# ScalarE takes the decode's gate sums and maxima out of the shared PSUM bank, and VectorE reads the copies

## The chip, the cores and the metric

The kernel runs on one NeuronCore of a Trainium2 chip. Its engines are TensorE (PE in the profile, with its weight loads as PEld), VectorE (DVE), ScalarE (ACT), GpSimd (POOL), which here mostly issues gathers, and SyncE (SP), which issues DMAs. Each engine works through its own instructions in order and waits at semaphores for the others. The metric is the device time of one execution in microseconds (us), the median of several runs; lower is better.

## What is computed

One step of a one-layer decoder for two groups that share their weights: a prompt of 1024 rows and a sample of 8 rows, each of which has 64 pages of 128 cached keys and values behind it. The work that the change touches is the forgetting attention of the sample over its cache:

```
c = jnp.cumsum(lf_all, axis=1)          # running sums of the forget gates' logs
s = jnp.einsum('bqhd,bkhd->bhqk', q, k) * (ATT_HEAD_DIM ** -0.5)
s = s + (cq - ck)                       # gate sum of the query less that of the key
p = jax.nn.softmax(s, axis=-1)
out = jnp.einsum('bhqk,bkhd->bqhd', p, v)
```

Around it the reference computes, for both groups, the input projection with RMSNorm, the prompt's causal attention with the same gates, a chunked spatial gating, an output projection, cross-attention into 256 memory rows, a gated MLP with a causal convolution, and the final norm; caches and states are returned too. All of it is float32.

## The kernel before

The prompt is the main line: input projection (`p1`), attention of rows 0 to 511 and of rows 512 to 1023 (`attention(0)`, `attention(1)`), then for each half output projection, cross-attention and MLP (`mid`, `ffn`). Float32 products are made of three matmuls on split operands (L272 to L274): ScalarE rounds a weight tile into `wh` (L235) and VectorE computes the rest `wl` (L236).

The sample's work is mixed into that line as a background generator, at a pace set per stage (`PACE`). `decode()` goes through 8 batches of 16 steps: a step gathers a 1 MB tile of keys through POOL (L1420), VectorE multiplies and sums it (L1436/L1440, or L1427/L1428 while the prompt's attention runs) into the scores `s`; two steps behind, the batch before gets its values gathered (L1482) and multiplied on TensorE (L1488). Keys and values share four `kv` buffers. Once for each batch:

- step 13: `gates` sums the gates. TensorE multiplies the page totals `tot` by a triangle (L1410) into a tile of 128x8, and VectorE makes the decay `dec` of 128x512 from that tile and the scanned gates `A` (L1412).
- step 15: `soft_max` adds `dec` to `s` (L1452) and takes each row's maximum `pm` (L1454).
- step 0 of the next batch: `soft_all` transposes `pm` (L1460), takes the maximum over all (L1463, L1464) and writes it on a diagonal `dg` (L1466).
- step 1 of the next batch: `soft_exp` spreads the maxima over the partitions with a matmul by ones (L1473) into a tile of 128x8, VectorE subtracts that tile from `s` (L1475), ScalarE takes the exponential (L1476) and VectorE sums it (L1477).

PSUM's eight banks are given out so: four `ba` and two `bb` for the main line, one `dv` for the decode's value sums, and one `ms`. `ms` holds a single buffer. The decode's small products (L1410, L1460, L1473) go there, and so does every third tile of the prompt attention's transposes and value products (`B3`: L836, L852, L872), which ScalarE copies out (L843, L861). A new tile in `ms` waits until all readers of the last one are done.

The order of instructions on each engine is made when the program is built: a planner simulates the engines' time and takes what is ready by priority. `tc.high_priority()` puts a block ahead of others in that choice; `behind(ENG.PE)` puts the decode's matmuls behind TensorE's newest instruction. At run time the order is fixed.

Of the kernel before, what the change touches and what calls it, by code (L numbers as in the profile page):

```python
# [11 lines left out]
AF = mybir.ActivationFunctionType  # L12
ALU = mybir.AluOpType
# [5 lines left out]
P = 128  # L19
# [59 lines left out]
def build(nc, tc, ctx, a, phases=None):  # L79
# [27 lines left out]
    def nm(s):  # L107
        cnt[0] += 1
        return f"{s}_{cnt[0]}"
# [16 lines left out]
    def sm(shape, tag, bufs=2, dt=F32):  # L126
        return small.tile(shape, dt, tag=tag, bufs=bufs, name=nm(tag))
# [24 lines left out]
    def MS():  # L152
        return BB() if MB else psum.tile([P, 512], F32, tag="ms", bufs=1, name=nm("ms"))
# [1207 lines left out]
    def behind(e):  # L1361

        return tc.issue_after(last[e]) if e in last else nullcontext()


    def decode():
# [36 lines left out]
        def gates(b, A):  # L1403
            tot = sm([P, 8], "tot", 2)
            nc.vector.tensor_tensor(
                tot, A.rearrange("p (h k) -> p h k", k=64)[:, :, 63], lfz[:, b * 8 : b * 8 + 8], op=ALU.add
            )
            ps = MS()
            with behind(ENG.PE):
                mmul(ps[:, :8], suf, tot, start=True, stop=True)  # L1410
            dt_ = dec("dec").rearrange("p (k h) -> p k h", h=8)
            nc.vector.tensor_tensor(  # L1412
                dt_, ps[:, :8].unsqueeze(1).broadcast_to((P, 64, 8)), A.rearrange("p (h k) -> p k h", k=64), op=ALU.subtract
            )
            return dt_

# [52 lines left out]
        def soft_exp(b, st, dg):  # L1469
            s = st[1]  # L1470
            ps = MS()
            with behind(ENG.PE):
                mmul(ps[:, :8], ones, dg, start=True, stop=True)  # L1473
            with tc.high_priority():
                nc.vector.tensor_tensor(s, s, ps[:, :8].unsqueeze(1).broadcast_to((P, 64, 8)), op=ALU.subtract)  # L1475
                nc.scalar.activation(s, s, AF.Exp)  # L1476
                nc.vector.tensor_reduce(lps[:, b, :], s.rearrange("p k h -> p h k"), axis=AX.X, op=ALU.add)  # L1477

# [38 lines left out]
        st, A, dt_, pm, dg, dv, vm = ([None] * 8 for _ in range(7))  # L1517
        pend = []
        st[0] = prep(0)
        for g in range(8 * 16 + 16 + VLAG + 2):  # L1520
# [5 lines left out]
            if ch == 1 and 1 <= b < 9:  # L1526
                soft_exp(b - 1, st[b - 1], dg[b - 1])
            left = 1
            if b < 8:
                left = yield from kstep(b, ch, st[b])  # L1530
                if ch == 11:
                    A[b] = gates_scan(b)
                if ch == 13:
                    dt_[b] = gates(b, A[b])
                if ch == 14 and b < 7:
                    st[b + 1] = prep(b + 1)
                if ch == 15:
                    pm[b] = soft_max(b, st[b], dt_[b])
# [486 lines left out]
```

## Time and profile before

| | us |
|---|---|
| runs of the kernel before: 1794.02, 1795.83, 1805.24; median | 1795.83 |
| the profiled execution's own time | 1805.72 |
| its span, first to last instruction | 1803.8 |
| TensorE busy in it | 1743.2 |
| VectorE busy | 1399.9 |
| ScalarE busy | 733.9 |
| GpSimd busy | 504.2 |

The profiled execution's time is its span and 1.92 us around it, and it lies 9.89 us above the median, near the longest of the three runs. By time of the span, the prompt's input projection ends near 275 us, the two attentions run from about 275 to 495 us, the first half's output projection, cross-attention and MLP follow to about 1100 us, and the second half's to the end. The decode's last value product is near 1416 us; after it comes the sample's own projection, cross-attention and MLP.

An answer of the trace gives for an instruction or a group its start, its duration, its engine and line, what it writes and reads, and in brackets the idle time of the engine just before it with what ended that. "x2" at a row's end means two instructions of the kind. A group's row has its count, its busy time and the mean of one in ns, then the engine's idle time before them by what ended it.

### The profile page before, as it was taken

To read this page: it belongs to the slowest core of one execution; us is meant where nothing else is said; L and a number is where in the kernel's file an instruction comes from. 1 tells how busy PE (TensorE), PEld (TensorE's weight loads), DVE (VectorE), ACT (ScalarE), POOL (GpSimd) and SP (SyncE) were. 2 spreads that over 40 slices of the span, in tenths; PEclk is the share of its full clock that TensorE was granted. 3 is DMA by queue.
4 is the path that set the end of the run, shared out by engine and by line. 5 is a ranking of instruction groups with operands and counts; after the bars stand their busy time and mean duration, and the time that the engine had idled before them with its cause. 6 is when DMAs were issued, how large, how long until landed. Compare 5 with 4: busy or idle time off the path is not lost.

```text
span 1803.8 us, 25097 instructions
## 1 busy us (share of the span) xinstructions
PE 1743.2 (97%) x9637; PEld 1291.8 (72%) x9637; DVE 1399.9 (78%) x1733; ACT 733.9 (41%) x1374; POOL 504.2 (28%) x461
## 2 busy tenths in 40 slices
PE   8999999878999999999999999999999999999997
PEld 5887777656677767777777777766666778767875
DVE  4689658987789897999999999887885549855344
ACT  6332256465634634433333244235353323332332
POOL 1252333432233433233232232433432112102110
PEclk9999999998999999999999999999999999999999
DMA  7886888786597986788788788988888677568982
GB/s 293 301 297 224 303 317 330 259 272 198 193 406 277 353 337 249 269 301 338 293 297 313 295 310 308 374 295 325 312 312 323 238 290 254 186 261 298 358 311 82
DMA packets 157074, 521.06 MB, mean 289 GB/s; under 512 B 20874, under 2 KB 40842, under 8 KB 124186
## 3 DMA queue, kind: packets, MB, share of 16 engines
q0 software_dynamic: 57168, 341.14, 50.0%
q1 hardware_dynamic: 92874, 165.73, 26.3%
q10 hardware_dynamic: 6912, 12.59, 1.9%
q8 instruction: 76, 1.25, 0.3%
q14 instruction: 44, 0.36, 0.1%
HBM read 495.47 MB, written 23.93 MB: 288 GB/s over the span
## 4 chain that ended last, share of the span: by engine, by line
PE 41%; issue 12%; DMA 10%; DVE 7%; POOL 4%; ACT 1%; POOLq 0%; DVEq 0%; ACTq 0%
DMA kv<-cache_v,io 7%; PE ba L272 6%; PE ba L274 6%; PE ba L273 6%; PE bb L272 3%; PE bb L274 3%; PE bb L273 3%; PE dv L1488 3%; DMA kv<-cache_k,io 2%; POOL kv L1420 2%; DVE s L1440 2%; DVE kv L1436 2%; POOL kv L1482 1%; PE dv L331 1%; PE dv L1764 1%
## 5 line engine op out<-in xcount | busy, mean ns | idle before, releaser
L235 ACT ACTIVATE wh<-wr 128x1024 fp32r<-128x1024 f32 (+2 forms) x220 | 228.6, 1043 | 421.2 <-PE ba L273 141.1
L236 DVE TENSOR_TENSOR wl<-wr,wh 128x1024 fp32r<-128x1024 f32 (+2 forms) x220 | 263.1, 1200 | 175.7 <-PE ba L274 58.0
L1420 POOL DMA_INDIRECT kv<-cache_k,io x128 | 193.2, 1509 | 574.5 <-DVE s L1440 325.7
L1436 DVE TENSOR_TENSOR kv<-kv,d 128x1024 f32<-128x1024 f32 (+1 forms) x156 | 258.1, 1681 | 21.6 <-DMA kv<-cache_k,io 21.4
L1440 DVE TENSOR_REDUCE s<-kv 128x16 f32<-128x1024 f32 (+1 forms) x156 | 258.1, 1673 | 0.0
L1482 POOL DMA_INDIRECT kv<-cache_v,io x128 | 171.0, 1336 | 254.8 <-PE dv L1488 179.2
L273 PE MATMUL ba<-u,wh 128*128 128x512 f32 x528 | 208.9, 396 | 0.5 <-DVE u L239 0.5
L272 PE MATMUL ba<-u,wh 128*128 128x512 f32 x528 | 209.2, 397 | 0.0
L274 PE MATMUL ba<-u,wl 128*128 128x512 f32 x528 | 209.0, 397 | 0.0
L272 PE MATMUL ba<-wh,u 128*128 128x512 f32 (+1 forms) x495 | 186.3, 379 | 0.9 <-ACT u L235 0.9
L273 PE MATMUL ba<-wl,u 128*128 128x512 f32 (+1 forms) x495 | 185.2, 375 | 1.2 <-DVE wl L236 1.2
L274 PE MATMUL ba<-wh,u 128*128 128x512 f32 (+1 forms) x495 | 183.2, 375 | 0.0
L1488 PE MATMUL dv<-kv,s 128*32 128x512 f32 x1024 | 127.1, 603 | 4.2 <-DMA kv<-cache_v,io 4.1
L274 PEld LDWEIGHTS ba<-u,wl 128*128 128x128 f32 x528 | 99.3, 188 | 27.2 <-issue 4.8
L272 PEld LDWEIGHTS ba<-u,wh 128*128 128x128 f32 x528 | 99.5, 188 | 26.4 <-issue 4.8
L273 PEld LDWEIGHTS ba<-u,wh 128*128 128x128 f32 x528 | 99.5, 188 | 26.0 <-issue 3.3
L272 PEld LDWEIGHTS ba<-wh,u 128*128 128x128 f32 x495 | 93.0, 188 | 25.0 <-issue 6.5
L272 PE MATMUL bb<-u,wh 128*128 128x512 f32 x272 | 108.5, 399 | 0.0
L274 PE MATMUL bb<-u,wl 128*128 128x512 f32 x272 | 107.9, 397 | 0.0
L273 PE MATMUL bb<-u,wh 128*128 128x512 f32 x272 | 107.7, 396 | 0.0
L273 PEld LDWEIGHTS ba<-wl,u 128*128 128x128 f32 x495 | 93.0, 188 | 20.2 <-DVE wl L236 2.1
L274 PEld LDWEIGHTS ba<-wh,u 128*128 128x128 f32 x495 | 92.9, 188 | 19.4 <-issue 1.6
(445 smaller groups left out, 3326.3 us busy)
## 6 DMA issues: line engine op xcount, KB each, us to landing
wr<-w_up SPq DMA_DIRECT2D x88, 512.0 KB
kv<-w_up POOLq DMA_DIRECT2D x22, 1024.0 KB, 9.0
wr<-w_down SPq DMA_DIRECT2D x40, 512.0 KB
kv<-w_down POOLq DMA_DIRECT2D x11, 1024.0 KB, 8.3
wr<-w_in SPq DMA_DIRECT2D x16, 512.0 KB
wr<-w_o SPq DMA_DIRECT2D x16, 512.0 KB
wr<-w_cq SPq DMA_DIRECT2D x16, 512.0 KB
wr<-w_co SPq DMA_DIRECT2D x16, 512.0 KB
```

What stands on the lines that cost most here:

```text
L235: nc.scalar.activation(h, src, AF.Copy)
L236: nc.vector.tensor_tensor(l, src, h.bitcast(F32), op=ALU.subtract)
L272: mmul(out, sh, mh, start=(i == 0), stop=False)
L273: mmul(out, sh, ml, start=False, stop=False)
L274: mmul(out, sl, mh, start=False, stop=(i == n - 1))
L331: mmul(ps[32 * j : 32 * j + 32, :w], xT[:, k, :] if nk == 8 else xT[:, k * 8 : k * 8 + 32], raw[:, q, j * w : (j + 1) * w], start=(k == 0) ...
L1420: nc.gpsimd.indirect_dma_start(kv, None, a["cache_k"], off(kidx[:, b, ch : ch + 1]))
L1436: nc.vector.tensor_tensor(kvv[:, i : i + m, :], kvv[:, i : i + m, :], qb.unsqueeze(1).broadcast_to((P, m, 512)), op=ALU.mult)
L1440: nc.vector.tensor_reduce(s[:, ch * 4 + i : ch * 4 + i + m, :].rearrange("p k h -> p (k h)"), kvv[:, i : i + m, :].rearrange("p k (h d) -> ...
L1482: nc.gpsimd.indirect_dma_start(kv, None, a["cache_v"], off(kidx[:, b, ch : ch + 1]))
L1488: mmul(dv[32 * j : 32 * j + 32, :], s[:, ch * 4 : ch * 4 + 4, :].rearrange("p k h -> p (k h)"), kvv[:, j, :], start=(ch == 1), stop=(ch == ...
L1764: mmul(ps[32 * j : 32 * j + 32, :P], xsT[:, k, :], rvs[j // 2][:, k, j % 2, :], start=(k == 0), stop=(k == 7), tile_position=(0, 32 * j),)
```

## The change

After each of the two matmuls by which the decode sums its gates and spreads its maxima, ScalarE copies the 128x8 result from `ms` into a small SBUF tile `sx` (two buffers), with high priority, and VectorE's instruction reads `sx` instead of the bank. Nothing else is edited. The maximum taken by L1463 still reads `ms`.

```diff
             ps = MS()
             with behind(ENG.PE):
                 mmul(ps[:, :8], suf, tot, start=True, stop=True)
+            sx = sm([P, 8], "sx", 2)
+            with tc.high_priority():
+                nc.scalar.activation(sx, ps[:, :8], AF.Copy)
             dt_ = dec("dec").rearrange("p (k h) -> p k h", h=8)
             nc.vector.tensor_tensor(
-                dt_, ps[:, :8].unsqueeze(1).broadcast_to((P, 64, 8)), A.rearrange("p (h k) -> p k h", k=64), op=ALU.subtract
+                dt_, sx.unsqueeze(1).broadcast_to((P, 64, 8)), A.rearrange("p (h k) -> p k h", k=64), op=ALU.subtract
             )
             return dt_
...
             ps = MS()
             with behind(ENG.PE):
                 mmul(ps[:, :8], ones, dg, start=True, stop=True)
+            sx = sm([P, 8], "sx", 2)
             with tc.high_priority():
-                nc.vector.tensor_tensor(s, s, ps[:, :8].unsqueeze(1).broadcast_to((P, 64, 8)), op=ALU.subtract)
+                nc.scalar.activation(sx, ps[:, :8], AF.Copy)
+                nc.vector.tensor_tensor(s, s, sx.unsqueeze(1).broadcast_to((P, 64, 8)), op=ALU.subtract)
                 nc.scalar.activation(s, s, AF.Exp)
                 nc.vector.tensor_reduce(lps[:, b, :], s.rearrange("p k h -> p h k"), axis=AX.X, op=ALU.add)
```

Since the planner places sixteen more instructions, the built program differs elsewhere too. TensorE, VectorE, GpSimd and SyncE have as many instructions as before and ScalarE has sixteen more; the loads of ScalarE's function tables stay at 20. The order moves in a few stretches: in the first attention around the two copies, near 435 to 447 us, near 715 to 805 us in the first MLP, and near 1195 to 1347 us, in the second half's cross-attention and output projection. From there to the end it is nearly that of before.

## The prediction

> **What bounds the kernel now.** I read the page's first part, then busy times by stage, then the groups that touch the bank `ms`, then the timeline at the places where TensorE waits for it.
>
> ```profile
> span 1803.8 us, 25097 instructions
> PE 1743.2 (97%) x9637; PEld 1291.8 (72%) x9637; DVE 1399.9 (78%) x1733; ACT 733.9 (41%) x1374; POOL 504.2 (28%) x461
> ```
>
> TensorE is busy 97% of the span, so all its waiting is 1803.8 - 1743.2 = 60.6 us, 3.4%. No change that leaves its matmuls alone, as this one does, can win more. Where the waiting lies is in the busy times by stage (columns: stretch; its length; busy PE, PEld, DVE, ACT, POOL; granted clock; DMA share; GB/s):
>
> ```profile
> 275.00:325.00 50.00, 47.12 (x262) 34.21 (x261) 44.21 (x70) 26.21 (x55) 21.76 (x29) 0.97 0.95 349
> 325.00:380.00 55.00, 47.35 (x305) 33.79 (x304) 45.01 (x101) 31.74 (x90) 21.65 (x30) 0.94 0.76 255
> 380.00:495.00 115.00, 102.32 (x684) 71.89 (x686) 94.57 (x156) 70.08 (x144) 31.48 (x42) 0.93 0.65 210
> 1060.00:1340.00 280.00, 269.59 (x1320) 194.77 (x1319) 244.79 (x275) 119.62 (x238) 99.80 (x69) 0.99 0.86 323
> ```
>
> The attentions (the first three rows) hold 2.9 + 7.7 + 12.7 = 23.2 us of it, and they alone share `ms` with the decode for long. The groups say how much of this is the decode's readers:
>
> ```profile
> L852 PE MATMUL ms<-t,u 128*64 128x256 f32 (+1 forms) x40 | 6.7, 379 | 3.9 <-DVE dec L1412 2.7 <-DVE s L1475 1.2
> L1412 DVE TENSOR_TENSOR dec<-ms,d 128x512 f32<-128x512 f32 x8 | 8.6, 1069 | 0.0
> L1475 DVE TENSOR_TENSOR s<-s,ms 128x512 f32<-128x512 f32 x8 | 5.4, 680 | 1.7 <-PE ms L1473 1.7
> L1452 DVE TENSOR_TENSOR s<-s,dec 128x512 f32<-128x512 f32 x8 | 5.5, 683 | 0.1
> L317 ACT ACTIVATE t<-ba 128x8 f32<-128x8 f32 x1 | 0.2, 173 | 0.0
> ```
>
> The first row is the heart of it. The prompt's value products in `ms` waited 2.7 us for L1412 and 1.2 us for L1475, once each: the decode is so slow that only one of its eight batches comes to these steps inside the attentions. The ceiling of what the two edits aim at is thus 3.9 us, 0.2% of the span.
>
> **Edit 1, the gate sums (L1410 to L1412).** The place, in time order:
>
> ```profile
> 313.98 0.34 PE L1410 MATMUL ms<-tot,cp 128*128 128x8 f32 x2
> 314.56 0.59 ACT L757 ACTIVATE u<-ba 64x512 fp32r<-64x512 f32 x1
> 314.60 2.28 POOL L758 CAST u<-u 64x512 fp32r<-64x512 f32 x2 [6.83 <-ACT u L757]
> 314.63 1.22 DVE L236 TENSOR_TENSOR wl<-wr,wh 128x1024 fp32r<-128x1024 f32 x1
> 315.18 0.38 ACT L843 ACTIVATE t<-bb 128x256 f32<-128x256 f32 x1
> 315.76 0.55 DVE L813 TENSOR_REDUCE mx<-ba 128x1 f32<-128x384 f32 x1
> 316.23 1.02 DVE L1412 TENSOR_TENSOR dec<-ms,d 128x512 f32<-128x512 f32 x1
> 317.31 1.55 PE L852 MATMUL ms<-t,u 128*64 128x256 f32 x8 [2.72 <-DVE dec L1412]
> ```
>
> The sums stood in the bank from 314.32. VectorE took them up at 316.23, behind a weight split and a maximum, and was done at 317.25; TensorE, with L852 next, idled 2.72 us. In the changed program's order the copy stands on ScalarE between the L757 that ended at 315.15 and the L843 shown. A copy of 128x8 out of PSUM takes 0.17 us (the row of L317), so the bank is free at 315.35. L843, pushed back by the copy, ends at 315.75 instead of 315.56. L852 reads what that L843 writes, so it can start near 315.8: 317.31 - 315.8 = 1.5 us won. The bounds: nothing, if VectorE's next steps are late for the scores behind L852; 2.72, the whole wait. I take 1.5, since both inputs are placed by rows.
>
> **Edit 2, the maxima (L1473 to L1475).** The same at 367 us:
>
> ```profile
> 366.83 0.29 PE L1473 MATMUL ms<-dg,ones 128*128 128x8 f32 x2
> 367.11 0.37 ACT L843 ACTIVATE t<-bb 128x256 f32<-128x256 f32 x1
> 367.26 0.55 PE L836 MATMUL bb<-cp,t 128*128 128x128 f32 x3
> 368.13 0.23 PE L811 MATMUL ba<-cmask_b,ident_b 128*128 128x128 bf16 x1
> 368.84 0.68 DVE L1475 TENSOR_TENSOR s<-s,ms 128x512 f32<-128x512 f32 x1
> 369.57 0.87 PE L852 MATMUL ms<-t,u 128*64 128x256 f32 x8 [1.21 <-DVE s L1475]
> ```
>
> TensorE finished L811 at 368.36 and waited 1.21 us. Changed, the copy follows the L843 that ended at 367.48, so the bank is free at 367.65; but the planner has also put L852 directly behind L1473, ahead of the L836 and the scores. TensorE then idles from 367.12 to about 367.7, 0.6 us, where it idled 0.14 (367.12 to 367.26) and 1.21 before. Won: 1.35 - 0.6 = 0.7 us, between 0 and 1.35.
>
> **What the edits add.** Sixteen copies of 0.17 us are 2.8 us on ScalarE, which is busy 41%. TensorE is fed by ScalarE through the weights' rounding:
>
> ```profile
> L235 ACT ACTIVATE wh<-wr 128x1024 fp32r<-128x1024 f32 (+2 forms) x220 | 228.6, 1043 | 421.2 <-PE ba L273 141.1 <-PE bb L273 78.3 <-PE ba L274 76.4
> ```
>
> Ahead of these 220, ScalarE idled 421 us, 1.9 us each, mostly until TensorE gave a buffer back: it runs ahead, and a copy of 0.17 us falls into that. I take 0 outside the attentions; with the cover gone it would be 2.8 us. VectorE's two instructions I leave at their time. L1452, of L1475's shape and with both inputs in SBUF, takes 683 ns against 680, so the bank is no slower to read than SBUF. L1412 might fall from 1069 towards that 683, 3.1 us in all, of which one instruction (0.4 us) is in the attentions; I take 0.
>
> A decode batch's chain gets two more hand-overs. Behind the copy on ScalarE's queue wait the next weights and the exponential, and TensorE's L1488 needs the exponential. The tightest place is batch 5:
>
> ```profile
> 1062.27 0.67 DVE L1475 TENSOR_TENSOR s<-s,ms 128x512 f32<-128x512 f32 x1
> 1066.08 1.25 ACT L1399 ACTIVATE d<-d 128x512 f32<-128x512 f32 x1 [4.62 <-DMA d<-cache_logf,lidx]
> 1068.64 0.63 ACT L1476 ACTIVATE s<-s 128x512 f32<-128x512 f32 x1
> 1069.18 1.04 ACT L235 ACTIVATE wh<-wr 128x1024 fp32r<-128x1024 f32 x1
> 1070.13 0.76 ACT L1297 ACTIVATE t<-ba,gp 128x512 f32<-128x512 f32 x1
> 1070.79 0.16 ACT L1298 ACTIVATE hlast<-ba 128x2 f32<-128x2 f32 x1
> 1071.54 1.50 PE L1488 MATMUL dv<-kv,s 128*32 128x512 f32 x12
> ```
>
> The scores were ready at 1062.94, but the exponential stood behind L1399, which waited for a gather, and ended at 1069.27, 2.3 us ahead of L1488. In the changed order L235, L1297 and L1298 (1069.18 to 1070.95, 1.8 us) come ahead of it too, and three matmuls (0.23 us each by the starts of neighbours) ahead of L1488. The margin shrinks to 2.3 - 1.8 + 0.7 = 1.2 us: hidden, but a gather that lands over 1.2 us later is paid for on TensorE. Elsewhere the copy costs a chain 0.2 us; bounded above by a copy behind one whole L235, 1.04 us, it stays under that margin.
>
> One more reader stood in TensorE's way, after the attentions:
>
> ```profile
> 1343.99 0.69 DVE L1475 TENSOR_TENSOR s<-s,ms 128x512 f32<-128x512 f32 x1 [0.96 <-PE ms L1473]
> 1344.73 0.17 PE L1606 MATMUL ms<-cp,mT 8*8 8x8 f32 x1 [0.78 <-DVE s L1475]
> ```
>
> Its 0.78 us could go. But the changed order puts that L1473 ahead of some eight short matmuls, where the diagonal it reads may not be ready, and TensorE would wait there. VectorE idled 0.96 us before L1475, so the diagonal was made by about 1343.03; the loss I bound by that 0.96. Between -0.8 and +1 us, I take 0.
>
> **The sum.** 1.5 + 0.7 = 2.2 us off 1805.72, 1803.5 for that execution. The median lies 9.89 us lower, and I carry the difference over: 1795.83 - 2.2 = 1793.6. As the later stages are TensorE's own work, an earlier end of the attentions goes through to the end.
>
> **A rule against it.** In edit 1's fence two POOL casts beside VectorE's L236, whose two inputs lie in SBUF, took 2.28 us, 1.14 each; this one, with VectorE at no such instruction when it began, took 0.63:
>
> ```profile
> 358.59 0.63 POOL L758 CAST u<-u 64x512 fp32r<-64x512 f32 x1
> ```
>
> POOL's spans are rough, but this looks like a hold-up of 0.5 us a cast. With the change L1412 and L1475 read two SBUF inputs as well: sixteen instructions, 8.6 + 5.4 = 14.0 us, with POOL busy 28% of the span, 3.9 us of POOL's time at most, and 1.02 + 0.68 = 1.7 us in the attentions, where the casts feed the scores. The Trainium skill (SBUF — State Buffer, section "Who interferes with whom") says that a VectorE instruction with two SBUF inputs contends with a GpSimd instruction that reads SBUF, which these casts bear out. Its time is the third rival's.
>
> **The rivals.**
> 1. Nothing is left (0.22). VectorE is busy 44.21 of 50 us where edit 1 stands; TensorE starts L852 earlier, then waits for maxima that VectorE makes no sooner. For it: most waits from 325 to 495 us are not for `ms`. Against: L813 ran ahead of L1412 anyway. Time 1795.8.
> 2. Slower by the queue (0.14). ScalarE, in order, holds a copy until TensorE has made the sum, with weights behind it; it decides where a copy waits longer than the 1.9 us that ScalarE is ahead. One place costs at most an L235 and the copy, 1.04 + 0.17 = 1.2 us; sixteen cost 19.4, 1815.2. Two to eight places are likelier, 1798 to 1805. Half of the 0.14 is for over 1%, as weights that come late once can be late again. Against it stands the idle time before L235.
> 3. POOL is held up (0.06): 1.7 of the 2.2 us lost, 1795.3.
> 4. The new order does more than the edits (0.08). TensorE waits 10.4 us of the stretch 1060 to 1340, where the order moves most. All of it and the 2.2 gone: 1783.2. Some 0.05 of this is for over 1%, since VectorE and the gathers move too and no row bounds them.
>
> **How the numbers follow.** The forecast keeps 0.50. A measurement of this kernel can tell about 1%, 18 us, from no change. Over 1% slower: 0.07. Over 1% faster: 0.05. Within 1%: 0.50 + 0.22 + 0.06 + 0.07 + 0.03 = 0.88. The range reaches down to 1784, nearly rival 4's full price, and up to 1805, eight places of rival 2 and also the longest run shown. It leaves out about 0.15.
>
> **What would show it.** Right: two rows of a ScalarE copy of 128x8 in the attentions, ending about 1 to 2 us ahead of VectorE's read; the waits of L852 for L1412 and L1475 gone and at most 0.6 us for the copy in place; L1412 and L1475 as long as before; L1488's wait for exponentials still nothing. Wrong: TensorE waiting for `sx` or for weights behind a copy; L1488 waiting for L1476 near 1071; longer casts; or a stage without copies that moves by more than the attentions do.

## The result and the profile after

The changed kernel takes 1808.82 us (median of 10 runs, 1805.27 to 1815.66) against 1799.22 us for the kernel before (median of 10, 1794.02 to 1805.24: the three runs shown at the start and seven more). The ratio is 1.006, with a 95% interval of 1.0047 to 1.0074: slower by about 10 us. The profiled execution took 1812.51 us, with a span of 1810.5.

The first line of the changed kernel's page:

```profile
PE 1741.6 (96%) x9637; PEld 1290.1 (71%) x9637; DVE 1400.1 (77%) x1733; ACT 735.5 (41%) x1390; POOL 514.3 (28%) x461
```

And from its groups those that answer to the ones shown of the kernel before, with two (the first rows) that are new to the story. "..." in a listing stands for rows left out. Line numbers have moved: the gate sums' reader L1412 is now L1415, the maxima's L1475 is L1480, the value product L1488 is L1493, the keys' gather L1420 is L1423, the products and sums of the scores L1436 and L1440 are L1439 and L1443; in some experiments they lie a few lines further on.

```profile
L273 PE MATMUL ba<-wl,u 128*128 128x512 f32 (+1 forms) x495 | 186.0, 377 | 5.4 <-DVE wl L236 5.4
...
L1180 PE MATMUL ba<-t,u 128*128 128x256 f32 x96 | 25.3, 418 | 9.3 <-ACT t L1167 9.3
...
L1415 DVE TENSOR_TENSOR dec<-sx,d 128x512 f32<-128x512 f32 x8 | 8.6, 1075 | 0.0
...
L852 PE MATMUL ms<-t,u 128*64 128x256 f32 (+1 forms) x40 | 6.9, 379 | 1.8 <-ACT sx L1413 1.4 <-ACT sx L1479 0.4
...
L1480 DVE TENSOR_TENSOR s<-s,sx 128x512 f32<-128x512 f32 x8 | 5.5, 682 | 0.3 <-ACT sx L1479 0.2
```

TensorE has the same matmuls and its waiting grew from 60.6 to 1810.5 - 1741.6 = 68.9 us. L852 lost its 3.9 us of waits for VectorE and has 1.8 us for the copies in their place; VectorE's two instructions take what they took. At the first edit's place little came of it in this execution:

```profile
319.95 1.06 ACT L235 ACTIVATE wh<-wr 128x1024 fp32r<-128x1024 f32 x1 [3.44 <-DMA wr<-w_cv]
320.91 0.37 ACT L843 ACTIVATE t<-ms 128x256 f32<-128x256 f32 x1
...
321.33 0.39 PE L1410 MATMUL ms<-tot,cp 128*128 128x8 f32 x2 [1.75 <-ACT t L843]
...
323.36 1.81 PE L852 MATMUL ms<-t,u 128*64 128x256 f32 x8 [1.37 <-ACT sx L1413]
```

A weight rounding L235 waits for its load, L843 stands behind it, and TensorE waits 1.75 us ahead of L1410 and 1.37 us ahead of L852: 3.12 us, where the kernel before waited 2.72. In experiments 3, 8, 9, 10 and 12, with the same order there, L1410 does not wait and L852 waits 0.82 us.

The first two rows of the groups hold the new waits. L273 now waits 5.4 us for weight splits, 4.10 us of it in the input projection, and the cross-attention's scores L1180 wait 9.3 us for ScalarE's L1167. Neither waits for a copy.

To see where the time went I cut each trace at the starts of the same matmuls, counted in TensorE's order from 0: the 820th (153.1 us in the kernel before), 1400th (276.0), 2300th (446.1), 5975th (1187.6) and 6740th (1350.5). The lengths of the stretches, in us, each a difference of two starts, the first from the first matmul on and the last up to the start of the last one:

| | to 820th | input projection | attentions | middle | second cross-attention | rest |
|---|---|---|---|---|---|---|
| before | 145.95 | 122.92 | 170.11 | 741.47 | 162.87 | 443.58 |
| after | 145.03 | 129.35 | 164.73 | 741.91 | 168.26 | 444.33 |

The attentions gained 5.4 us in this pair of executions (more on this below), and two stretches that the edits did not aim at lost 6.4 and 5.4 us.

**The second cross-attention.** The timeline of the kernel before, ScalarE's rows and the one of TensorE's L1180, which starts without a wait:

```profile
1244.87 1.06 ACT L235 ACTIVATE wh<-wr 128x1024 fp32r<-128x1024 f32 x1
1245.82 0.59 ACT L1226 ACTIVATE u<-bb 128x512 f32<-128x512 f32 x1
1246.30 0.60 ACT L1167 ACTIVATE t<-ba 128x512 f32<-128x512 f32 x1
1246.78 0.61 ACT L1201 ACTIVATE u<-ba 128x512 f32<-128x512 f32 x1
...
1246.95 3.72 PE L1180 MATMUL ba<-t,u 128*128 128x256 f32 x16
...
1247.57 1.06 ACT L235 ACTIVATE wh<-wr 128x1024 fp32r<-128x1024 f32 x1 [0.19 <-DMA wr<-w_co]
```

And of the changed kernel:

```profile
1246.32 1.99 ACT L235 ACTIVATE wh<-wr 128x1024 fp32r<-128x1024 f32 x2
1248.52 1.70 ACT L1193 ACTIVATE u<-u,cr 128x256 f32<-128x256 f32 x4 [0.22 <-DVE cr L1191]
1253.65 1.06 ACT L235 ACTIVATE wh<-wr 128x1024 fp32r<-128x1024 f32 x1 [3.42 <-DMA wr<-w_co]
1254.61 0.58 ACT L1226 ACTIVATE u<-bb 128x512 f32<-128x512 f32 x1
1255.09 0.59 ACT L1167 ACTIVATE t<-ba 128x512 f32<-128x512 f32 x1
...
1255.73 6.57 PE L1180 MATMUL ba<-t,u 128*128 128x256 f32 x16 [9.33 <-ACT t L1167]
```

The planner has turned the order round: four L1193 and a rounding L235 whose weights are still on their way now stand ahead of L1167, and TensorE needs what L1167 writes. The kernel before has a wait of its own a little later, 3.59 us of a value product for its gather, which is gone. That wait is not in every execution of the old order: in experiments 2, 3, 5 and 8 it is L1180 that waits 2.4 us instead. The sixteen matmuls also take 6.57 us instead of 3.72, of which more below.

**The input projection.** Timeline of the changed kernel near 150 us:

```profile
149.91 9.51 POOL L1423 DMA_INDIRECT kv<-cache_k,io  x1 [1.25 <-DVE cc L537]
...
150.56 1.08 DVE L1415 TENSOR_TENSOR dec<-sx,d 128x512 f32<-128x512 f32 x1
...
151.91 6.68 DVE L1439 TENSOR_TENSOR kv<-kv,d 128x2048 f32<-128x2048 f32 x3
158.51 2.27 DVE L1443 TENSOR_REDUCE s<-kv 128x32 f32<-128x2048 f32 x1
164.43 2.29 DVE L1439 TENSOR_TENSOR kv<-kv,d 128x2048 f32<-128x2048 f32 x1 [3.65 <-DMA kv<-cache_k,io]
166.64 1.22 DVE L236 TENSOR_TENSOR wl<-wr,wh 128x1024 fp32r<-128x1024 f32 x1
...
167.91 0.79 PE L273 MATMUL ba<-wl,u 128*128 128x512 f32 x1 [4.10 <-DVE wl L236]
```

Near 150 us the order of all engines is that of the kernel before; only batch 0's gate sums come from `sx`. The gather L1423 took GpSimd 9.51 us, until 159.42. It had 0.65 us before L1415 began, 0.3 us between L1415 and L1439, and ended 0.83 us after the last L1439 did. Its keys came late, L1439 waited 3.65 us for them, the weight split L236 stands behind that, and TensorE behind the split. The same gather in the kernel before took 1.22 us, with L1412, reading the bank, beside it:

```profile
150.11 0.67 DVE L236 TENSOR_TENSOR t<-t,t 8x512 fp32r<-8x512 f32 x1
...
150.39 1.22 POOL L1420 DMA_INDIRECT kv<-cache_k,io  x1 [1.25 <-DVE cc L537]
...
151.04 1.08 DVE L1412 TENSOR_TENSOR dec<-ms,d 128x512 f32<-128x512 f32 x1
```

The small L236, which has two SBUF inputs too, stands ahead in both kernels and covers 0.39 us of the gather's start. Behind its end the gather of the kernel before needed 0.83 us; in the changed kernel L1415 began 0.26 us behind it.

### The profile page after: what moved, and what is told of

Same layout as the page of the kernel before. It is cut to its first block, busy times and chain, and to the rows that moved or that the text cites. A ratio compares the mean times of both kernels' runs of the same rounds, so it can differ in the third digit from the quotient of the medians.

```text
span 1810.5 us, 25115 instructions
## 1 busy us (share of the span) xinstructions
PE 1741.6 (96%) x9637; PEld 1290.1 (71%) x9637; DVE 1400.1 (77%) x1733; ACT 735.5 (41%) x1390; POOL 514.3 (28%) x461
## 4 chain that ended last, share of the span: by engine, by line
PE 53%; DMA 9%; DVE 7%; issue 7%; ACT 3%; POOL 1%; POOLq 0%; DVEq 0%; ACTq 0%; SPq 0%
PE ba L272 6%; PE ba L274 6%; PE ba L273 6%; DMA kv<-cache_v,io 4%; PE dv L1493 4%; DMA kv<-cache_k,io 3%; PE bb L272 3%; PE bb L274 3%; PE bb L273 3%; DVE s L1443 2%; DVE kv L1439 2%; PE ba L1066 1%; PE dv L331 1%; PE ba L1065 1%; PE ba L1064 1%
## 5 line engine op out<-in xcount | busy, mean ns | idle before, releaser
L235 ACT ACTIVATE wh<-wr 128x1024 fp32r<-128x1024 f32 (+2 forms) x220 | 228.5, 1043 | 440.8 <-PE ba L273 139.1
L236 DVE TENSOR_TENSOR wl<-wr,wh 128x1024 fp32r<-128x1024 f32 (+2 forms) x220 | 263.1, 1200 | 171.6 <-PE ba L274 57.6
L1423 POOL DMA_INDIRECT kv<-cache_k,io x128 | 207.0, 1617 | 568.4 <-DVE s L1443 336.9
L1439 DVE TENSOR_TENSOR kv<-kv,d 128x1024 f32<-128x1024 f32 (+1 forms) x156 | 258.1, 1681 | 31.5 <-DMA kv<-cache_k,io 31.5
L1443 DVE TENSOR_REDUCE s<-kv 128x16 f32<-128x1024 f32 (+1 forms) x156 | 258.3, 1674 | 0.0
L273 PE MATMUL ba<-u,wh 128*128 128x512 f32 x528 | 208.8, 395 | 0.5 <-DVE u L239 0.5
L273 PE MATMUL ba<-wl,u 128*128 128x512 f32 (+1 forms) x495 | 186.0, 377 | 5.4 <-DVE wl L236 5.4
L1493 PE MATMUL dv<-kv,s 128*32 128x512 f32 x1024 | 127.3, 599 | 0.0
L273 PEld LDWEIGHTS ba<-u,wh 128*128 128x128 f32 x528 | 99.2, 188 | 26.7 <-issue 4.0
L273 PEld LDWEIGHTS ba<-wl,u 128*128 128x128 f32 x495 | 93.6, 189 | 23.8 <-DVE wl L236 6.3
L273 PE MATMUL bb<-u,wh 128*128 128x512 f32 x272 | 107.9, 397 | 0.0
```

The costliest lines, as they stand in the source:

```text
L235: nc.scalar.activation(h, src, AF.Copy)
L236: nc.vector.tensor_tensor(l, src, h.bitcast(F32), op=ALU.subtract)
L273: mmul(out, sh, ml, start=False, stop=False)
L1423: nc.gpsimd.indirect_dma_start(kv, None, a["cache_k"], off(kidx[:, b, ch : ch + 1]))
L1439: nc.vector.tensor_tensor(kvv[:, i : i + m, :], kvv[:, i : i + m, :], qb.unsqueeze(1).broadcast_to((P, m, 512)), op=ALU.mult)
L1443: nc.vector.tensor_reduce(s[:, ch * 4 + i : ch * 4 + i + m, :].rearrange("p k h -> p (k h)"), kvv[:, i : i + m, :].rearrange("p k (h d) -> ...
```

## The experiments

To part the order from the copies, most kernels have their order written in: after the program is traced, each engine's instructions are chained in a stored order, and only the copies (listed in `free`) are left to the planner. This part is the same in each, and only the table ORDER differs:

```diff
+    for e in (ENG.PE, ENG.DVE, ENG.Activation, ENG.Pool, ENG.SP):
+        mine = [i for i in ins if i.engine == e and "Boundary" not in type(i).__name__]
...
+        for _ in range(n):
+            at_ += 1 + number()
+            if prev is not None:
+                tc.add_manual_dep(
+                    mine[at_], prev.name, mybir.DependencyInfo(mybir.DependencyClass.NoSync, mybir.DependencyReason.DATA)
+                )
+            prev = mine[at_]
```

Experiments 1 to 4, 5 to 8 and 9 to 12 each ran beside runs of the kernel before, with medians of 1801.56, 1800.77 and 1800.38 us; each ratio is to those runs.

### Order against copies

**1. Old instructions, new order** (the kernel before, chained in the changed program's order).

> The kernel before, without a single copy, but each engine's instructions chained in the order in which the changed program has them. Theory (the order costs it: in the changed program's order ScalarE's weight rounding that waits for a late load stands ahead of the cross-attention's L1167, and TensorE idles 9 us there): 8 to 11 us slower than the kernel before, with an idle time of TensorE of 8 to 10 us ahead of the cross-attention's scores L1180 near 1256 us. Rival (the sixteen copies and their hand-overs cost it): within 2 us of the kernel before, since there is no copy.

Ratio 1.0044 (1.0027 to 1.0061), L1180's wait 8.54 us. Without one copy, most of the loss is there, a little less than the 8 to 11 us of the theory.

**2. All copies, old order** (the changed kernel, chained in the order of before).

> The changed kernel with all sixteen copies, but each engine's other instructions chained in the order that the kernel before has; the copies alone are placed by the planner. Theory (the order costs it): 0 to 4 us faster than the kernel before, the two waits of L852 for VectorE (2.72 and 1.21 us) shorter or gone. Rival (the copies and hand-overs cost it): 8 to 11 us slower, as the changed kernel is.

Ratio 1.002 (1.0006 to 1.0034). Both expectations missed: the copies cost some 3 us in the old order as well, where I expected a gain, but a third of what the rival says. L852's waits fell from 2.72 and 1.21 us to 0.82 and nothing that shows; the wait for `wl` near 166 us is there with 2.53 us.

**3. All copies, new order up to about 1150 us, old order from there.**

> The changed kernel with all copies and its own order up to about 1150 us; from there (second half's cross-attention on) the order of the kernel before. Theory: the L1180 wait of 9.3 us goes and the 3.6 us wait of a value product for its gather near 1258 us comes back, so 4 to 6 us less than the changed kernel, which leaves 3 to 6 us over the kernel before. Rival (copies): no change from the changed kernel, 8 to 11 us over.

Ratio 1.0003 (0.9989 to 1.0016). Putting the late part of the order back removes the whole loss that can be told, some 10 us by the two ratios and more than the 4 to 6 us expected. L1180 waits 2.43 us, and the value product's wait of 3.6 us did not come back.

**4. No copies, new order only from about 1150 us on.**

> The kernel before without copies, its own order up to about 1150 us and the changed program's order from there. Theory: 4 to 7 us slower than the kernel before, with the wait of 8 to 10 us ahead of L1180. Rival (copies): within 2 us of it.

Ratio 1.0041 (1.0024 to 1.0057), L1180's wait 8.69 us. The late part alone costs what the whole new order cost in the first experiment, as the theory says.

### What the copies cost by themselves

**5. Copies made, but read by nobody** (old order; VectorE reads the bank). The gate sums' half of the edit, the maxima's is alike:

```diff
-            sx = sm([P, 8], "sx", 2)
+            cx = sm([P, 8], "sx", 2)
             with tc.high_priority():
-                nc.scalar.activation(sx, ps[:, :8], AF.Copy)
+                free.append(nc.scalar.activation(cx, ps[:, :8], AF.Copy).ins)
+            sx = ps[:, :8]
```

> All sixteen copies are made by ScalarE, but VectorE still reads the bank, so the copies are used by nobody; order of the kernel before. Theory (the copies' own cost, 3 us in the second kernel, comes from VectorE's instruction that now reads two SBUF inputs and holds up a GpSimd gather near 150 us, which takes 9.5 instead of 1.2 us): that gather is back at 1.2 us, TensorE's wait of 2.5 to 4.1 us for wl near 166 us is gone, and the time is 0 to 1.5 us over the kernel before. Rival (the copies' places in ScalarE's queue cost it): 2 to 4 us over the kernel before.

Ratio 1.0008 (0.9991 to 1.0024). Its timeline at the gather:

```profile
148.69 1.21 POOL L1424 DMA_INDIRECT kv<-cache_k,io  x1 [1.25 <-DVE cc L537]
...
149.35 1.07 DVE L1416 TENSOR_TENSOR dec<-ms,d 128x512 f32<-128x512 f32 x1
```

ScalarE makes all sixteen copies, and the gather is back at 1.21 us; no wait for `wl` follows. The copies' places in ScalarE's queue cost nothing that can be measured. What costs is that VectorE reads `sx`.

**6. Copies for batch 1 alone** (old order), the batch that meets the attentions; at the gates:

```diff
-            sx = sm([P, 8], "sx", 2)
-            with tc.high_priority():
-                nc.scalar.activation(sx, ps[:, :8], AF.Copy)
+            if b == 1:
+                sx = sm([P, 8], "sx", 2)
+                with tc.high_priority():
+                    free.append(nc.scalar.activation(sx, ps[:, :8], AF.Copy).ins)
+            else:
+                sx = ps[:, :8]
```

> Only batch 1, the one that meets the attentions, has its two copies; the other batches read the bank; order of the kernel before. Theory: 0 to 3 us faster than the kernel before, as the two waits of L852 shrink and no gather is held at 150 us; if the scores behind L852 are as late as before, no change. Rival (each copy costs at its place): 0.2 to 0.5 us slower, two sixteenths of 3 us.

Ratio 0.999 (0.9976 to 1.0004): a gain of some 2 us, not parted from none by the interval. What takes the place of the waits, from its timeline:

```profile
313.88 0.18 ACT L1414 ACTIVATE sx<-ms 128x8 f32<-128x8 f32 x1
...
314.11 1.14 PE L852 MATMUL ms<-t,u 128*64 128x256 f32 x8 [0.82 <-ACT sx L1414]
...
329.79 0.55 PE L836 MATMUL bb<-cp,t 128*128 128x128 f32 x3 [2.00 <-ACT t L814]
```

L852 starts 1.9 us earlier for its place, as soon as the copy is done and before the L843 behind it ends, and 15 us on TensorE waits 2.00 us for an exponential L814 that VectorE's maxima make no sooner.

**7. One copy, batch 0's gate sums** (the same edit with b == 0, at the gates alone; old order).

> Only the copy of batch 0's gate sums is made and read; all else reads the bank; order of the kernel before. Theory: this one copy holds the gather at 9.5 us and opens the wait for wl near 165 us, 2.5 to 4 us slower than the kernel before. Rival (the cost lies evenly on sixteen copies): 0.2 us, not to be measured.

Ratio 1.0029 (1.0015 to 1.0042): one copy of sixteen costs 4 to 5 us, a little over the 2.5 to 4 expected and all that the sixteen together cost in the second experiment. The gather takes 9.49 us and TensorE waits 2.22 us for `wl`.

**8. As the third, but batch 0's gate sums read from the bank** (b > 0 at the gates).

> As the third kernel (all copies, the changed program's order up to about 1150 us, the order of the kernel before from there), but batch 0's gate sums are read from the bank. Theory: 2.5 to 4 us less than the third kernel, 2 to 4 us faster than the kernel before. Rival (evenly): as the third kernel, no change from the kernel before.

1798.51 us, ratio 0.9986 (0.9974 to 0.9999): with both causes out, the copies and the new order up to 1150 us together are some 2.3 us faster than the kernel before, as expected, with an interval that just leaves out no change. It is the fastest of the tried kernels against its own baseline, by little.

### What in the late order

**9. The changed kernel, nine instructions of ScalarE put back** (ORDER differs in nine places: L1226, L1167 and an L1201 ahead of L235, the four L1193 behind).

> The changed kernel with all copies in its own order, except nine instructions of ScalarE near 1249 to 1257 us in the order that the kernel before has: L1226, L1167 and a L1201 ahead of the weight rounding L235 that waits for its load, and four L1193 behind. Theory (that rounding in front of L1167 makes the 9.3 us wait of L1180): the wait falls to 1 to 4 us and the kernel is 4 to 7 us faster than the changed one, 3 to 6 us over the kernel before. Rival (VectorE's order, which makes the scales and the weight splits later, would hold L1167 and the maxima just the same): no more than 2 us from the changed kernel, 8 to 10 us over.

Ratio 1.003 (1.0017 to 1.0044), L1180's wait 1.50 us: as the theory says. Its timeline:

```profile
1248.56 0.59 ACT L1167 ACTIVATE t<-ba 128x512 f32<-128x512 f32 x1
1249.04 0.60 ACT L1201 ACTIVATE u<-ba 128x512 f32<-128x512 f32 x1
...
1249.21 3.72 PE L1180 MATMUL ba<-t,u 128*128 128x256 f32 x16 [1.50 <-ACT t L1167]
...
1253.50 1.06 ACT L235 ACTIVATE wh<-wr 128x1024 fp32r<-128x1024 f32 x1 [3.86 <-DMA wr<-w_co]
```

L235 waits for its weights as in the changed kernel, but L1167 is out of its way. The stretch from the 5975th matmul to the 6740th falls from 168.26 us to 164.13, where the old order has some 161. Another 2.17 us of waiting for L1167 appears at 1262.57; the 3 us that are left were not followed further.

**10. The changed kernel, VectorE's order near 1242 to 1253 us put back** (a run of thirteen instructions, of which eleven change their place in ORDER).

> The changed kernel in its own order, except thirteen instructions of VectorE near 1242 to 1253 us in the order of the kernel before, which puts two weight splits L236 ahead of the scores' products, so that the weight buffers come free some 2 to 4 us earlier; ScalarE's order stays the changed one. Theory (the load behind those splits is what ScalarE's L235 waits for): the wait ahead of L1180 falls by 2 to 4 us, 2 to 4 us off the changed kernel. Rival (the load is late for another cause): no change from the changed kernel.

Ratio 1.0054 (1.004 to 1.0068), no change that can be told, and L1180 still waits 8.57 us. The theory was right on the load and wrong on the wait:

```profile
1243.24 2.01 ACT L235 ACTIVATE wh<-wr 128x1024 fp32r<-128x1024 f32 x2
1247.13 1.70 ACT L1193 ACTIVATE u<-u,cr 128x256 f32<-128x256 f32 x4 [1.88 <-DVE cr L1191]
1248.74 1.04 ACT L235 ACTIVATE wh<-wr 128x1024 fp32r<-128x1024 f32 x1
...
1250.17 0.58 ACT L1167 ACTIVATE t<-ba 128x512 f32<-128x512 f32 x1
```

The weights now come in time, and TensorE still idles: L1167 stands behind L1193, which waits for VectorE, and behind three L235. With the ninth kernel, what counts is what stands ahead of L1167, not which of it is late.

**11. Batch 1's copies, order as in the third.**

> Only batch 1 has its two copies; the changed program's order up to about 1150 us, that of the kernel before from there. Theory: as the eighth kernel or 1 us better, 2 to 4 us faster than the kernel before, since the fourteen copies left out gained nothing. Rival (the copies of other batches gain too): slower than the eighth kernel by over 1 us.

Ratio 0.9995 (0.9981 to 1.0009). The 2 to 4 us expected were not there; its interval overlaps that of the eighth kernel, so which of the two is better stays open.

**12. Batch 1's copies, ordered by the planner.**

> Only batch 1 has its two copies and nothing is chained: the planner orders all, as in the changed kernel. From about 1150 us on its order is that of the changed program but for a few places. Theory (the late order costs it, whatever made the planner choose it): 4 to 8 us slower than the kernel before, with the wait of some 9 us ahead of L1180. Rival (the number of copies decides): within 2 us of the kernel before.

Ratio 1.0044 (1.0026 to 1.0062), L1180's wait 8.49 us, as the theory says. Two copies near 315 and 367 us are enough for the planner to turn ScalarE's order round at 1250 us.

## Why the prediction was wrong

The stretches of all fourteen profiled executions, grouped by what the kernel has, give the account (means; in brackets lowest and highest, and the count):

| stretch | without | with | difference |
|---|---|---|---|
| input projection, batch 0's gate sums from `sx` | 122.9 (122.8 to 123.1, 8) | 127.3 (124.9 to 129.4, 6) | +4.4 |
| attentions, old order, batch 1's copies read | 169.2 (168.3 to 170.1, 4) | 167.3 (167.1 to 167.6, 2) | -1.8 |
| attentions, new order, batch 1's copies read | 167.4 (1) | 165.3 (163.8 to 168.0, 7) | -2.1 |
| middle, new order up to 1150 us (twelfth left out) | 740.6 (739.7 to 741.5, 6) | 742.0 (741.1 to 743.3, 7) | +1.4 |
| second cross-attention, new late order (ninth left out) | 161.2 (157.5 to 162.9, 8) | 168.0 (167.6 to 168.5, 5) | +6.9 |
| rest, new late order (ninth left out) | 443.7 (443.6 to 443.8, 8) | 444.4 (444.3 to 444.7, 5) | +0.7 |

The new order of the attentions is worth another 169.2 - 167.4 = 1.8 us without a copy, by one execution. With the copies' 2.1 us in that order the sum is 4.4 - 1.8 - 2.1 + 1.4 + 6.9 + 0.7 = +9.5 us, near the 9.6 us between the medians; it could have missed by more, as the executions of one group differ by up to 5 us. What the new order does in the middle was not looked into.

The forecast had 2.2 us less, all of it in the attentions, and 0 elsewhere.

- **The two edits: right in size, in part by luck.** I forecast 2.2 us; at equal order the attentions gained 1.8 and 2.1, the second against one execution without copies that lies within the range of those with them. The rows show the copies where they were put. L852 waits 1.37 and 0.42 us for them, where I had allowed 0.6, and in the sixth kernel it won 1.9 us at its place for the 1.5 forecast. But the first rival's wait for later scores is there too, and in the old order the waiting did not shrink in all. The attentions in busy times, of the kernel before, the changed, the fifth (copies unread) and the sixth:

```profile
275.97:446.08 170.11, 149.42 (x904) 106.85 (x904) 145.85 (x262) 94.34 (x218) 63.81 (x87) 0.92 0.80 271
```

```profile
281.48:446.21 164.73, 144.11 (x903) 102.69 (x904) 144.69 (x262) 93.50 (x218) 64.33 (x88) 0.96 0.84 280
```

```profile
274.66:442.94 168.28, 146.56 (x904) 104.14 (x905) 145.38 (x262) 93.79 (x219) 64.85 (x87) 0.94 0.80 273
```

```profile
274.77:441.83 167.06, 145.47 (x904) 103.63 (x905) 145.33 (x262) 93.97 (x219) 64.07 (x87) 0.95 0.81 275
```

TensorE idles 20.7, 20.6, 21.7 and 21.6 us of them (length less busy PE): as long with the copies read as without. What got shorter is its busy time, with a higher granted clock (0.92 against 0.96, 0.94 against 0.95), and the sum had no term for the clock. In the new order the waits may have shrunk: in the first kernel, without copies, L852 waits 3.54 and 2.54 us and TensorE idles 25.3 us in all, in the seven with them 20.6 to 25.0. That the rest of the attentions' order gives 1.8 us more, I had put at nothing.

- **The ceilings of 60.6 and 3.9 us: not a bound.** I took TensorE's waits for all that could be won. The gains at equal order stayed under 3.9 us, but 5.4 us went from the attentions in the first pair with the waiting unchanged. A wait can also slow the matmuls behind it, which the profile counts as busy, as the last section shows.
- **VectorE's readers "at their time": right, and beside the point.** L1415 takes 1075 ns against 1069, L1480 682 against 680. I asked what the second SBUF input does to VectorE, but its price falls on GpSimd.
- **The rule against the change, and rival 3: right mechanism, wrong victim and size.** I priced it on casts in the attentions, 1.7 us, against the edits' gain. The casts do pay (two L758 take 3.14 us in the sixth kernel, with the reader of `sx` beside them, though in the changed kernel none takes over 0.66), but the instruction that paid was one gather at 150 us, 8.3 us of GpSimd's time and 4.4 us of the stretch. I had bounded all sixteen readers by 3.9 us of GpSimd's time, their own length by its busy share; the gather was held much longer than its reader ran, since L1439 follows it. And I had searched only the attentions for it. The profile of before shows such a hold-up outright:

```profile
161.19 2.27 DVE L1436 TENSOR_TENSOR kv<-kv,d 128x2048 f32<-128x2048 f32 x1
161.53 3.96 POOL L1420 DMA_INDIRECT kv<-cache_k,io  x1 [9.33 <-DVE s L1440]
163.38 1.21 DVE L236 TENSOR_TENSOR wl<-wr,wh 128x1024 fp32r<-128x1024 f32 x1
164.52 2.27 DVE L1440 TENSOR_REDUCE s<-kv 128x32 f32<-128x2048 f32 x1
```

The gather begins beside L1436, seems to get nowhere while that and L236 read two SBUF inputs, and ends at 165.49, 0.97 us after the one-input L1440 began; the gather at 148.20, with no such instruction beside it, took 0.95 us in all. The reader of the gate sums was, in the kernel before, the one-input gap in which batch 0's gather got through; with `sx` it became part of a wall of 8 us with one gap of 0.3.

- **Copies on ScalarE at nothing: right.** The fifth kernel has them all and costs 0.08%, with an interval that holds no change. Batch 5's exponential, whose margin I put at 1.2 us, ended at 1071.66, and L1493 waited 0.0 us for it. In the old order rival 2 thus fell.
- **"Later stages are TensorE's own work", and rival 4: the step that failed.** The sum had nothing for the new order behind the attentions, and ScalarE's lead of 1.9 us ahead of each L235 stood as cover. I had said that the order moves most from 1060 to 1340 us, and priced that only as a gain, up to the 10.4 us that TensorE waits there. The runs showed the opposite sign: the late order alone, without a copy, costs some 7 us (fourth kernel) and opens a wait of 8.7 us ahead of L1180. In the changed order, putting nine instructions of ScalarE back is enough to bring that wait from 9.33 down to 1.50 us (ninth kernel); no kernel had ScalarE's order alone changed in the old program. The lead says nothing of an L235 that stands in front of an instruction TensorE is waiting for. I had the order of the changed program and could have walked this stretch, asking of each instruction that moved up what it waits for and who stands behind it. The input projection's 4.4 us are the other term that the sum put at nothing: it left VectorE's two readers at their time. Of the signs that I gave for being wrong, the waiting for `sx` was there, but small, and two stretches that the edits did not aim at moved by as much as the attentions or more, though copies stand in both.

Why the planner turns that order round is not settled: the twelfth kernel shows that two copies some 900 us earlier suffice, not by what rule.

## What to carry to other kernels

Where a scheduler places the instructions, an edit has two effects, its own and that of the new order; write the old order in and run the edit alone, and the new order without the edit, and the two come apart. Moving an operand from PSUM to SBUF can make VectorE's instruction one with two SBUF inputs, which held up GpSimd's gathers here: look at what GpSimd does beside each such instruction. Of the sixteen here one cost 4 to 5 us, the others nothing that could be told. Before calling a moved instruction free, read what it waits for and what stands behind it on its engine.

## What was not expected of the hardware

**A gather is held up while VectorE reads two SBUF inputs.** With the gate sums' reader reading `sx`, the gather near 149 us took 9.49 to 9.51 us wherever it was shown (the changed kernel, experiments 2, 3, 7, 9, 10), and 1.21 to 1.22 us in each of the eight others. The Trainium skill (SBUF — State Buffer, section "Who interferes with whom") has the contention with GpSimd instructions that read SBUF, which agrees: a gather reads the indices of its rows from SBUF. It infers that such an instruction leaves descriptor generation (the making of a DMA's list of transfers) alone. The loads that GpSimd issues without indices agree with that:

```profile
1667.87 1.43 POOL L1558 DMA_DIRECT2D kv<-w_up  x2 [5.41 <-PE dv L1764]
...
1668.56 0.69 DVE L236 TENSOR_TENSOR wl<-wr,wh 128x512 fp32r<-128x512 f32 x1 [2.42 <-PE ba L273]
```

The second of the two loads lies beside L236 and takes 0.72 us, as the first does without it; all 22 of these loads in the kernel before take 0.72 to 0.73. So it is the gather that is held, and the reading of its indices fits; no run shows that apart.

**Behind a wait of some 2 us TensorE's clock can be halved.** Granted clock (the column after POOL's busy time) in the changed kernel, behind the wait for `wl`:

```profile
168.00:172.00 4.00, 4.00 (x10) 3.13 (x11) 4.00 (x3) 0.30 (x1) 1.67 (x1) 0.50 0.45 131
```

and in the second kernel, behind a wait of 2.53 us:

```profile
166.41:168.91 2.50, 2.50 (x11) 2.06 (x12) 2.50 (x2) 0.00 (x0) 0.09 (x1) 1.00 0.49 125
```

In the first, with the wait of 4.10 us, the stretch is 6.4 us longer; the 4 us shown at 0.50 account for some 2 us of that, by an estimate from these rows. In the seventh kernel 2.22 us was enough for a clock of 0.50, so the length of the wait alone does not decide it. The kernel before has 0.50 from 1187.3 to 1190.3 us too, next to a wait of 1.69 us. Behind L1180's wait the clock was 0.50 too, and sixteen matmuls took 6.57 instead of 3.72 us. The Trainium skill (TensorE: Matmul & The Clock Gate, Part 1) has a clock that falls to half after an idle window and a window that runs freely; its 3.4 us of idling is more than the 2.22 seen here, where the measurement decides, while a free-running window would fit the 1.00 after 2.53. In the attentions it works for the change: over 317 to 325 us the kernel before has 0.80, its wait of 2.72 us just ahead, and the sixth kernel, with that wait down to 0.82 us, 1.00. The five kernels in which batch 1's copies are not read have 0.60 to 0.84 there, seven of the nine in which they are have 1.00. The other two are the changed kernel, with 0.87 and the two waits shown, and the eleventh, with 0.63 and a wait of 1.37 us.

```profile
317.00:325.00 8.00, 7.69 (x36) 5.97 (x37) 7.91 (x12) 1.70 (x4) 3.46 (x5) 0.80 0.93 330
```

```profile
317.00:325.00 8.00, 8.00 (x44) 5.16 (x43) 7.94 (x12) 1.34 (x3) 3.57 (x5) 1.00 1.03 375
```
